# The attention part of y in DRAM, the pool part added by DMAs that add, and y's tiles lent to other rings

## The chip, the cores and the metric

The kernel runs on one core of a Trainium2 chip. The metric is the device time of one execution in microseconds (us); each kernel is judged by the median of its runs. Each core has five engines that take their instructions in order and meet at semaphores: TensorE (PE; its weight loads are listed as PEld), VectorE (DVE), ScalarE (ACT), GpSimd (POOL) and SyncE (SP), which here only issues DMAs. GpSimd issues some DMAs on a queue of its own.

## The reference

A DeepNorm decoder layer on 2048 rows of 1024 features, in float32. What matters here is its second half: an attention branch and a pooling branch, each projected to 1024 features, gated by sigmoids, added, projected again and normalised.

```python
  u = x * (1 + scale) + shift
  [q | k | v | a_gate | p_in | p_gate | m_a | m_p] = u @ W_in
  a = (attention(q, k, v) * silu(a_gate)) @ W_attn_proj
  p = (group_linear(causal_pool(p_in)) * pool_scale * silu(p_gate)) @ W_pool_proj
  y = sigmoid(m_a) * a + sigmoid(m_p) * p
  y = (y @ W_out) * (1 + gate)
  x = layer_norm(alpha * x + y)
```

## The kernel before

**How a product is made.** Every float32 operand is split into a high half that TensorE takes exactly and a low half, and a product is three: high by high, high by low, low by high (`mm3`). On top of that, two by two blocks of each large product are multiplied by a scheme with seven products in place of eight. A `Quad` is one such block: two weight tiles as the stationary side (loaded into `W` and `A22`, combined on GpSimd in `sum1`, `mid` and `late`, split by `pair_split` and `half_split` with the high half on ScalarE, L315, and the low half on VectorE, L131), and seven prepared "sets" B11, T1, T2, B21, T3, B22, T4 as the moving side. One product is 12 matmuls of 128x512, so a quad is 84 matmuls. `front` makes B11 and T1 of a quad, `back` the rest; the sums of products (u2, p5, c12) are made on VectorE and GpSimd (L366, L387). Four times in a quad a finished 128x512 result goes to the quad's `consume`, with (mi, t) saying which of the two weight tiles and which half of 1024 rows it belongs to.

**Stages.** Gates are computed first (stages g0 and g1, one for each half s of the rows) and written to DRAM, among them `ma_d` (sigmoid of m_a) and `mp_d`. Attention of a half follows each (a0 and a1); its result is stored as sets `ain_d` in DRAM. The last stage, called mix, starts with what was opened in a1 and has five phases: attention projection of s=0, pool projection of s=0, both again for s=1 (four quads each, in two groups of two), and the output projection with the normalisation of rows (eight quads).

**Tiles of the mix stage.** `Pools("mix", spare=2, p=4, c=5)` gives rings of 128x512 tiles (c with five places, p with four) and of 128x1024 tiles (spare with two). Eight tiles `wide0` to `wide7` of 128x1024 hold the attention part of y for the eight feature tiles, `ta[k]`; `wide4` to `wide7` are taken at the stage's start. In the output phase the same wide tags hold gain, bias and rows of x.

**Consumers.** `attn_quad` takes a place of ring c for the gate (ga), loads it on SP (L541), and VectorE multiplies the product by it into the half of `ta[k]` (L544). `pool_quad` loads its gate (gp, L551), VectorE multiplies in place (L552), GpSimd adds it to `ta` (L554), and GpSimd's queue stores the sum to `y_d` (L556), with 512-byte rows. Output quads load rows of `y_d` as their weights.

**Order of work.** Instructions written through `sp`, `act`, `dve`, `pool` and `pe` keep the order of the program on their engine; those through `nc.sync`, `nc.vector`, `nc.scalar` and `nc.gpsimd` are placed by a scheduler. A `tick` is called once per product; `defer(n, f)` runs f n ticks later, and `hooks` name work by group and tick. `set_steps` spreads the loading (SP, into a spare tile) and splitting (ACT and DVE) of the next phase's sets over fourteen half sets at the ticks of `SPLIT_AT`, with two loads ahead of the splits.

Of the kernel before, what the change touches and what calls it, by code (L numbers as in the profile page):

```python
# [2 lines left out]

# [1 line left out]

# [13 lines left out]
P = 128  # L19
# [39 lines left out]
def kernel(  # L59
# [84 lines left out]
    class Pools:  # L144


        def __init__(self, name, **bufs):
            self.name, self.bufs = name, bufs

        def __enter__(self):  # L150
            self.stack = ExitStack()
# [14 lines left out]
            return wp.tile([P, D], F32R, tag="wset", bufs=4, name="w_set")  # L166

        def spare(self, dt=F32):
            return self.t.tile([P, D], dt, tag="spare", bufs=self.bufs["spare"], name="spare")

        def c(self, name="c", dt=F32, tag="c"):
            return self.t.tile([P, CH], dt, tag=tag, bufs=self.bufs[tag], name=name)

        def p(self, name):
# [90 lines left out]
    class Quad:  # L265
# [1 line left out]

        def __init__(self, srcs, consume):  # L270
            self.srcs, self.consume = srcs, consume

        def load(self, ph, own, q=nc.sync, e=nc.gpsimd):
            self.w, self.a22 = ph.weights(), ph.last(own)
# [77 lines left out]
    def back(ph, grp, opened, nxt, own, tick, b22_first=False):  # L352
        st = []
        for q, (a, b, c, w) in zip(grp, opened):
            u2, p5 = ph.p("u2"), ph.p("p5")
            nc.scalar.copy(u2, a)
            nc.scalar.copy(p5, b)
            if w is None:
                w = pair_split(ph, q.second())
                q.late()  # L360
            if c is None:
                c = bank("lg")
                product(c, w[1], "T2", True)
            tick()
            nc.vector.tensor_tensor(u2, c, u2, ALU.add)  # L365
            nc.gpsimd.tensor_tensor(p5, p5, u2, ALU.add)  # L366
# [10 lines left out]

        def third(x):
            w[x] = pair_split(ph, st[x][0].third())
            if x < len(nxt):  # L380
                ask(nxt[x])

# [25 lines left out]
                with_b22(x)  # L408
        for q in nxt[len(st) :]:
            ask(q)  # L410
        for q, b, c, u2, p5 in st:
            w = half_split(ph, q.a22)
            product(c, w, "T4")
            tick()
            nc.vector.tensor_tensor(u2, c, u2, ALU.add)  # L415
            q.consume(ph, 1, 0, u2)
# [3 lines left out]
    def defer(ticks, f):  # L420
        due.append((now[0] + ticks, len(due), f))
# [48 lines left out]
    def set_steps(ph, store):  # L470


        if store["B11"].shape[0] == 4:
            return [(p, lambda n=n, h=h: fill_set(n, h, store[n])) for p, n, h in PLAN]
        raw, todo = {}, []

        def fetch(k):
            name, half = PLAN[k][1:]
            raw[k] = ph.spare()
            sp.dma_start(raw[k], store[name][half].rearrange("p a b -> p (a b)"))  # L480

        def split(k):
            name, half = PLAN[k][1:]
            split_set(name, 2 * half, by_two(raw[k]), 2, (act, dve))

        for k, at in enumerate(SPLIT_AT):
            if k < 2:
                todo.append((0, lambda k=k: fetch(k)))
            todo.append((at, lambda k=k: split(k)))
            if k + 2 < len(SPLIT_AT):  # L490
                todo.append((at, lambda k=k: fetch(k + 2)))
        return todo

    def planned(hooks, ph, store, last, pending={}):
# [39 lines left out]
    def wide(ph, i):  # L534
        return ph.t.tile([P, D], F32, tag=f"wide{i}", bufs=1, name=f"wide{i}")

    def attn_quad(s, m):
        def consume(ph, mi, t, src):
            k = m + mi
            g = ph.c("ga")  # L540
            nc.sync.dma_start(g, gates_d["ma"][s, k, t])  # L541
            if k not in ta:
                ta[k] = wide(ph, k)
            nc.vector.tensor_tensor(ta[k][:, t * CH : (t + 1) * CH], src, g, ALU.mult)  # L544

        return Quad((wap[m], wap[m + 1]), consume)

    def pool_quad(s, m):
        def consume(ph, mi, t, src):
            g = ph.c("gp")  # L550
            nc.sync.dma_start(g, gates_d["mp"][s, m + mi, t])  # L551
            nc.vector.tensor_tensor(g, src, g, ALU.mult)  # L552
            dst = ta[m + mi][:, t * CH : (t + 1) * CH]
            nc.gpsimd.tensor_tensor(dst, g, dst, ALU.add)  # L554
            k = 8 * s + 4 * t
            nc.gpsimd.dma_start(  # L556
                y_d[k : k + 4, :, m + mi, :].rearrange("s p q -> p s q"), dst.rearrange("p (s q) -> p s q", s=4)
            )

        return Quad((wpp[m], wpp[m + 1]), consume)  # L560

    zs = {}

# [756 lines left out]
        opened = attention(ph, 1, q0, (ain0_d, attn0[0]))  # L1320
    kv_stack.close()

    ta, vec = {}, {}
    with Pools("mix", spare=2, p=4, c=5) as ph:
        late_sets(ph.t, "T3", "T4")
        for k in range(4, KT):
            ta[k] = wide(ph, k)
        phases = []
        for s in range(2):
            phases.append((pairs(lambda m, s=s: attn_quad(s, m)) if s else attn0, ain_d[s]))  # L1330
# [3 lines left out]
        for i, (groups, store) in enumerate(phases):  # L1334
# [79 lines left out]
```

## Time and profile before

| | us |
|---|---|
| median of 3 runs | 1825.05 |
| lowest and highest | 1823.41 and 1826.09 |
| the profiled execution | 1824.69 |
| its span | 1822.9 |
| mean granted TensorE clock | 0.983 of full speed |

The span is what the profiler's rows cover. A row of the page names an engine, its busy time, its share of the span and its count of instructions. A row of the timeline gives a start, the time it took, the engine, the line, the operation with its tiles (output, arrow, inputs), a count, and in brackets the idle time before it and what ended that. A row of a group gives the sum and mean of its instructions and the idle time ahead of them. A row of DMA issues names the transfer, the queue that issues it, the count, the size of one and the median time from issue to landing. A row of waits names the instruction that waited, what it waited for, the total, the number of times and the longest.

### The profile page before, as it was taken

To read this page: it belongs to the slowest core of one execution; us is meant where nothing else is said; L and a number is where in the kernel's file an instruction comes from. 1 tells how busy PE (TensorE), PEld (TensorE's weight loads), DVE (VectorE), ACT (ScalarE), POOL (GpSimd) and SP (SyncE) were. 2 spreads that over 40 slices of the span, in tenths; PEclk is the share of its full clock that TensorE was granted. 3 is DMA by queue.
4 is the path that set the end of the run, shared out by engine and by line. 5 is a ranking of instruction groups with operands and counts; after the bars stand their busy time and mean duration, and the time that the engine had idled before them with its cause. 6 is when DMAs were issued, how large, how long until landed. Compare 5 with 4: busy or idle time off the path is not lost. (4 is left out here: it accounts for less than half of the span.)

```text
span 1822.9 us, 25301 instructions
## 1 busy us (share of the span) xinstructions
PE 1722.4 (94%) x8248; PEld 1432.9 (79%) x8248; DVE 1315.4 (72%) x2290; ACT 933.8 (51%) x1965; POOL 929.5 (51%) x758
## 2 busy tenths in 40 slices
PE   6789899999999999999999999999989999999996
PEld 6678787878888887777777888888877778777775
DVE  6967676644777787787666467777848897877887
ACT  4644344445777776444444377777724343423451
POOL 2245454551356567635445125357744875576552
PEclk9899999999999999999999999999999999999998
DMA  9265667656344468676676724453876575688442
GB/s 358 94 213 184 224 218 236 241 208 168 122 162 145 165 223 299 234 262 242 243 262 236 254 80 148 156 172 129 300 271 220 196 254 184 211 312 349 150 156 87
DMA packets 164003, 381.32 MB, mean 209 GB/s; under 512 B 19728, under 2 KB 23840, under 8 KB 163872
## 3 DMA queue, kind: packets, MB, share of 16 engines
q1 hardware_dynamic: 150528, 342.17, 53.7%
q0 software_dynamic: 10112, 33.06, 5.2%
q10 hardware_dynamic: 3232, 4.49, 0.9%
q8 instruction: 65, 1.06, 0.2%
q14 instruction: 66, 0.54, 0.1%
HBM read 244.35 MB, written 138.44 MB: 210 GB/s over the span
## 5 line engine op out<-in xcount | busy, mean ns | idle before, releaser
L55 PE MATMUL mm<-set_B,w_set 128*128 128x512 f32 x3240 | 802.1, 396 | 22.2 <-DVE w_set L131 22.0
L55 PEld LDWEIGHTS mm<-set_B,w_set 128*128 128x128 f32 x3240 | 602.9, 189 | 154.0 <-DVE w_set L131 30.3
L55 PE MATMUL lg<-set_T,w_set 128*128 128x512 f32 x2088 | 521.9, 400 | 44.3 <-DVE w_set L131 16.7
L55 PEld LDWEIGHTS lg<-set_T,w_set 128*128 128x128 f32 x2088 | 396.0, 192 | 146.2 <-DVE w_set L131 27.0
L131 DVE TENSOR_TENSOR w_set<-W,w_set 128x1024 fp32r<-128x1024 f32 x162 | 241.9, 1493 | 130.3 <-ACT w_set L315 125.6
L315 ACT CAST w_set<-W 128x1024 fp32r<-128x1024 f32 x162 | 169.2, 1049 | 242.5 <-PE mm L55 134.1
L55 PE MATMUL mm<-set_T,w_set 128*128 128x512 f32 x1080 | 266.4, 395 | 0.0
L55 PEld LDWEIGHTS mm<-set_T,w_set 128*128 128x128 f32 x1080 | 201.3, 189 | 41.6
L293 POOL TENSOR_TENSOR W<-W 128x512 f32<-128x512 f32 x56 | 80.0, 1429 | 151.0 <-DVE w_set L131 142.3
L287 POOL TENSOR_TENSOR W<-W 128x512 f32<-128x512 f32 x56 | 87.2, 1556 | 125.2 <-DVE w_set L131 99.9
L366 POOL TENSOR_TENSOR p<-p,u 128x512 f32<-128x512 f32 x58 | 100.6, 1736 | 87.3 <-DVE u L365 79.4
L55 DVE TENSOR_TENSOR o<-pv,o 64x128 f32<-64x128 f32 x256 | 72.4, 283 | 93.2 <-ACT o L55 90.5
L55 ACT ACTIVATE L<-L,nm 128x257 f32<-128x257 f32 (+1 forms) x256 | 127.1, 498 | 8.4 <-DVE nm L55 3.3
L283 POOL TENSOR_TENSOR W<-W,A 128x512 f32<-128x512 f32 x56 | 82.7, 1476 | 86.9 <-DMA W<-in_win_dram 20.2
L55 DVE TENSOR_TENSOR k_lo<-spare,k_hi 128x512 fp32r<-128x512 f32 x88 | 92.4, 1058 | 47.8 <-ACT k_hi L55 24.0
L55 DVE CUSTOM_DVE_ANT_0 L<-lg,bt,nsink 128x256 f32<-128x256 f32 (+1 forms) x256 | 111.6, 473 | 5.3 <-PE lg L55 1.3
L288 POOL TENSOR_TENSOR W<-W 128x512 f32<-128x512 f32 x56 | 90.4, 1614 | 15.1 <-DMA W<-in_win_dram 12.3
L55 POOL TENSOR_TENSOR w_set<-W,w_set 128x1024 fp32r<-128x1024 f32 x14 | 33.7, 2405 | 122.8 <-ACT w_set L55 89.7
L55 POOL TENSOR_TENSOR p<-nxt,pg 128x512 f32<-128x512 f32 x32 | 41.3, 1291 | 104.6 <-DVE sm L55 104.6
L55 ACT COPY o<-pv 64x256 f32<-64x256 f32 x128 | 47.3, 370 | 82.3 <-PE pv L55 80.2
L55 DVE TENSOR_TENSOR ptl<-pt,pth 128x512 fp32r<-128x512 f32 (+1 forms) x128 | 85.7, 669 | 1.7 <-ACT pth L55 1.6
L55 ACT CAST k_hi<-spare 128x512 fp32r<-128x512 f32 x88 | 53.4, 615 | 60.4 <-POOL spare L55 32.3
(207 smaller groups left out, 2507.2 us busy)
## 6 DMA issues: line engine op xcount, KB each, us to landing
W<-in_win_dram SPq DMA_DIRECT2D x68, 256.0 KB, 4.1
w_set<-wmix_d SPq DMA_DIRECT2D x32, 512.0 KB, 5.4
A<-in_win_dram SPq DMA_DIRECT2D x34, 256.0 KB, 5.1
W<-in_win_dram POOLq DMA_DIRECT2D x34, 256.0 KB, 3.6
ag_d<-sig SPq DMA_DIRECT2D x32, 256.0 KB, 3.5
pg_d<-sig SPq DMA_DIRECT2D x32, 256.0 KB, 3.6
ma_d<-sig SPq DMA_DIRECT2D x32, 256.0 KB, 4.1
mp_d<-sig SPq DMA_DIRECT2D x32, 256.0 KB, 3.7
```

The costliest lines, as they stand in the source:

```text
L55: return lambda *args, **kw: self.tc.keep_in_program_order(op(*args, **kw))
L131: engine.tensor_tensor(dst, src, as32(hi), ALU.subtract)
L283: e.tensor_tensor(self.w[:, 1, :], self.w[:, 2, :], self.a22, ALU.add)
L287: e.tensor_tensor(x[:, 1, :], x[:, 1, :], x[:, 0, :], ALU.subtract)
L288: e.tensor_tensor(x[:, 2, :], x[:, 0, :], x[:, 2, :], ALU.subtract)
L293: e.tensor_tensor(x[:, 0, :], x[:, 0, :], x[:, 1, :], ALU.subtract)
L315: a.copy(by_two(hi), raw)
L366: nc.gpsimd.tensor_tensor(p5, p5, u2, ALU.add)
```

## The change

The attention part of y no longer stays in SBUF. Both kinds of quad become one, `mixer_quad`. It loads the gate into a place of ring c (`gm`) with an ordered SP DMA at a time of its own, `ask`, which `Quad` now has beside `consume`: for result (0, 0) ahead of the T2 product, for the two results of t = 1 when the weights of T3 and B22 are split, and for (1, 0) ahead of the T4 products. `consume` multiplies the product by the gate in place. For attention it then stores the tile to `y_d` with a plain SP DMA two ticks later; for the pool part GpSimd's queue issues a DMA that adds the tile to what `y_d` holds (`accum_op=ALU.add`). The GpSimd add and `ta` are gone.

The eight wide tiles are lent: `wide0` to `wide3` to ring c, which so has nine places, taken in turn, and `wide4` to `wide7` to ring spare, which so has six. In the second pool phase, at tick 12 of its first group, the loan ends, and the tiles serve the output phase as before. The set loads run five ahead of the splits in place of two.

```diff
+        def lend(self, c, spare):
+            self.rooms = {"c": cycle(self.bufs["c"] * [None] + c), "spare": cycle(self.bufs["spare"] * [None] + spare)}
+
+        def room(self, ring):
+            return next(self.rooms[ring]) if self.rooms else None
...
         def spare(self, dt=F32):
+            tag = self.room("spare")
+            if tag:
+                return self.t.tile([P, D], dt, tag=tag, bufs=1, name="spare")
             return self.t.tile([P, D], dt, tag="spare", bufs=self.bufs["spare"], name="spare")
 
         def c(self, name="c", dt=F32, tag="c"):
+            room = self.room("c") if tag == "c" else None
+            if room:
+                return self.t.tile([P, D], dt, tag=room, bufs=1, name=name)[:, 0:CH]
             return self.t.tile([P, CH], dt, tag=tag, bufs=self.bufs[tag], name=name)
...
-        def __init__(self, srcs, consume):
-            self.srcs, self.consume = srcs, consume
+        def __init__(self, srcs, consume, ask=None):
+            self.srcs, self.consume, self.ask = srcs, consume, ask or (lambda *a: None)
...
                 w = pair_split(ph, q.second())
                 q.late()
+            q.ask(ph, 0, 0)
             if c is None:
                 c = bank("lg")
                 product(c, w[1], "T2", True)
...
         def third(x):
             w[x] = pair_split(ph, st[x][0].third())
+            for mi in ((0, 1) if b22_first else (1, 0)):
+                st[x][0].ask(ph, mi, 1)
             if x < len(nxt):
                 ask(nxt[x])
...
         for q in nxt[len(st) :]:
             ask(q)
+        for q, *_ in st:
+            q.ask(ph, 1, 0)
         for q, b, c, u2, p5 in st:
             w = half_split(ph, q.a22)
             product(c, w, "T4")
...
         for k, at in enumerate(SPLIT_AT):
-            if k < 2:
-                todo.append((0, lambda k=k: fetch(k)))
+            if k < 5:
+                todo.append((k // 2, lambda k=k: fetch(k)))
             todo.append((at, lambda k=k: split(k)))
-            if k + 2 < len(SPLIT_AT):
-                todo.append((at, lambda k=k: fetch(k + 2)))
+            if k + 5 < len(SPLIT_AT):
+                todo.append((at, lambda k=k: fetch(k + 5)))
...
+    def mixer_quad(s, m, weights, name):
+        gates = {}
+
+        def ask(ph, mi, t):
+            g = gates[mi, t] = ph.c("gm")
+            sp.dma_start(g, gates_d[name][s, m + mi, t])
+
+        def consume(ph, mi, t, src):
+            g = gates.pop((mi, t))
+            nc.vector.tensor_tensor(g, src, g, ALU.mult)
+            k = 8 * s + 4 * t
+            dst = y_d[k : k + 4, :, m + mi, :].rearrange("s p q -> p s q")
+            part = g.rearrange("p (s q) -> p s q", s=4)
+            if name == "ma":
+                defer(2, lambda: sp.dma_start(dst, part))
+            else:
+                nc.gpsimd.dma_start(dst, part, accum_op=ALU.add)
+
+        return Quad((weights[m], weights[m + 1]), consume, ask)
...
     def attn_quad(s, m):
-        def consume(ph, mi, t, src):
-            k = m + mi
-            g = ph.c("ga")
-            nc.sync.dma_start(g, gates_d["ma"][s, k, t])
-            if k not in ta:
-                ta[k] = wide(ph, k)
-            nc.vector.tensor_tensor(ta[k][:, t * CH : (t + 1) * CH], src, g, ALU.mult)
-
-        return Quad((wap[m], wap[m + 1]), consume)
+        return mixer_quad(s, m, wap, "ma")
 
     def pool_quad(s, m):
-        def consume(ph, mi, t, src):
-            g = ph.c("gp")
-            nc.sync.dma_start(g, gates_d["mp"][s, m + mi, t])
-            nc.vector.tensor_tensor(g, src, g, ALU.mult)
-            dst = ta[m + mi][:, t * CH : (t + 1) * CH]
-            nc.gpsimd.tensor_tensor(dst, g, dst, ALU.add)
-            k = 8 * s + 4 * t
-            nc.gpsimd.dma_start(
-                y_d[k : k + 4, :, m + mi, :].rearrange("s p q -> p s q"), dst.rearrange("p (s q) -> p s q", s=4)
-            )
-
-        return Quad((wpp[m], wpp[m + 1]), consume)
+        return mixer_quad(s, m, wpp, "mp")
...
-    ta, vec = {}, {}
+    vec = {}
     with Pools("mix", spare=2, p=4, c=5) as ph:
         late_sets(ph.t, "T3", "T4")
-        for k in range(4, KT):
-            ta[k] = wide(ph, k)
+        ph.lend(["wide0", "wide1", "wide2", "wide3"], ["wide4", "wide5", "wide6", "wide7"])
...
-            if i in (2, 4):
-                ta.clear()
             if i == 3:
...
+                hooks.setdefault((0, 12), []).append(lambda: ph.lend([], []))
                 hooks.setdefault((-1, 5), []).append(vectors)
                 hooks.setdefault((-1, 7), []).append(lambda: [load_z(ph, row) for row in range(2)])
```

More of the change, by code (lines that the diff above doesn't have):

```diff
@@ L2 @@
 from contextlib import ExitStack
+from itertools import cycle
 import numpy as np
@@ L148, in __init__ @@
             self.name, self.bufs = name, bufs
+            self.rooms = None
+        def lend(self, c, spare):
+            self.rooms = {"c": cycle(self.bufs["c"] * [None] + c), "spare": cycle(self.bufs["spare"] * [None] + spare)}
+        def room(self, ring):
+            return next(self.rooms[ring]) if self.rooms else None
         def __enter__(self):
```

## The prediction

> **What bounds the kernel now.** I read the page's busy shares first, then busy times by stage, then TensorE's timeline inside the stage that the change touches, then who holds up what TensorE waits for. The profiled execution took 1824.69 us (span 1822.9, so 1.8 around it), 0.36 below the median of the runs shown; the sum below is made against 1824.69 and nothing is added for that 0.36.
>
> ```profile
> PE 1722.4 (94%) x8248; PEld 1432.9 (79%) x8248; DVE 1315.4 (72%) x2290; ACT 933.8 (51%) x1965; POOL 929.5 (51%) x758
> ```
>
> TensorE is busy 94%, so a change that touches no matmul can only take from the remaining 6% and from clock lost. The diff lies in the last stage alone. Its attention phase s=0 ends at 1394.96, its pool phase at 1481.05, the attention and pool phases of s=1 at 1561.49 and 1642.81, and the output projection near 1801.60. In the windows the columns are stretch, length, busy time of PE, PEld, DVE, ACT, POOL, granted clock, DMA share, GB/s.
>
> ```profile
> 1325.51:1394.96 69.45, 64.02 (x268) 51.41 (x266) 43.12 (x48) 22.19 (x26) 31.08 (x22) 0.95 0.70 252
> 1394.96:1481.05 86.09, 79.01 (x336) 63.89 (x337) 77.60 (x63) 33.10 (x39) 63.69 (x50) 0.98 0.65 221
> 1481.05:1561.49 80.44, 78.08 (x336) 64.12 (x337) 65.08 (x63) 32.63 (x39) 43.69 (x30) 0.98 0.60 208
> 1561.49:1642.81 81.32, 77.44 (x334) 62.15 (x335) 65.78 (x54) 24.71 (x30) 56.91 (x47) 1.00 0.77 273
> 1642.81:1801.60 158.79, 150.70 (x651) 122.62 (x650) 124.12 (x159) 65.45 (x98) 85.11 (x66) 0.99 0.52 194
> ```
>
> Each middle phase is 336 matmuls. What would they take without a gap? TensorE's timeline has a run of twelve groups of 12 with no idle time between them:
>
> ```profile
> 1325.51 11.42 PE L55 MATMUL mm<-set_B,w_set 128*128 128x512 f32 x48
> 1336.76 5.60 PE L55 MATMUL lg<-set_T,w_set 128*128 128x512 f32 x24
> 1346.01 8.69 PE L55 MATMUL lg<-set_T,w_set 128*128 128x512 f32 x24 [3.65 <-ACT w_set L315]
> 1354.55 2.88 PE L55 MATMUL mm<-set_B,w_set 128*128 128x512 f32 x12
> ...
> 1387.18 5.60 PE L55 MATMUL lg<-set_T,w_set 128*128 128x512 f32 x24
> 1394.96 2.60 PE L55 MATMUL mm<-set_B,w_set 128*128 128x512 f32 x10 [1.72 <-DVE w_set L131]
> 1436.27 3.63 PE L55 MATMUL mm<-set_B,w_set 128*128 128x512 f32 x10 [2.35 <-DVE w_set L131]
> 1474.74 2.98 PE L55 MATMUL lg<-set_T,w_set 128*128 128x512 f32 x12 [1.62 <-DVE p L387]
> 1481.05 3.98 PE L55 MATMUL mm<-set_B,w_set 128*128 128x512 f32 x10 [2.88 <-DVE w_set L131]
> 1561.49 2.60 PE L55 MATMUL mm<-set_B,w_set 128*128 128x512 f32 x10 [2.37 <-DVE w_set L131]
> ```
>
> From 1354.55 to 1387.18 is 32.63 us for 144 matmuls, 226.6 ns each, so a phase has a floor of 336 x 0.2266 = 76.1 us. Over it the first pool phase loses 86.09 - 76.1 = 10.0, the attention phase of s=1 4.3, the second pool phase 5.2. Those 19.5, and the start of the stage (gap 3.65, then 24 matmuls in 8.69 where the same 24 take 5.60 at 1387.18: 6.7 together), are all that the change can win: 26 us. Nearly every gap is ended by VectorE, by the low half of a weight split (L131) or a product sum (L387): VectorE is late, though busy only some 80 to 90% of a phase.
>
> **Why VectorE is late** has two parts in the trace. The first is GpSimd's adds:
>
> ```profile
> 1619.14 1.23 DVE L131 TENSOR_TENSOR w_set<-W,w_set 128x1024 fp32r<-128x1024 f32 x1 [6.35 <-ACT w_set L315]
> 1626.67 5.75 DVE L131 TENSOR_TENSOR w_set<-W,w_set 128x1024 fp32r<-128x1024 f32 x1 [0.22 <-ACT w_set L315]
> 1626.30 1.30 POOL L366 TENSOR_TENSOR p<-p,u 128x512 f32<-128x512 f32 x1
> 1627.55 1.29 POOL L283 TENSOR_TENSOR W<-W,A 128x512 f32<-128x512 f32 x1
> 1628.80 1.29 POOL L554 TENSOR_TENSOR wide<-gp,wide 128x512 f32<-128x512 f32 x1
> 1630.05 1.28 POOL L288 TENSOR_TENSOR W<-W 128x512 f32<-128x512 f32 x1
> ```
>
> The same subtraction takes 1.23 alone and 5.75 while GpSimd runs four tensor operations end to end; it ends when they do. One of the four is the add L554, which the change removes; its price over all is in the group row, and what L131 takes in the phases with and without many of these adds is in the windows of that line (stretch, length, busy and count):
>
> ```profile
> L554 POOL TENSOR_TENSOR wide<-gp,wide 128x512 f32<-128x512 f32 x32 | 47.3, 1479 | 9.3 <-DVE gp L552 8.9
> 1394.96:1481.05 86.09, 29.35 (x16) 0.98 0.65 221
> 1481.05:1561.49 80.44, 22.08 (x16) 0.98 0.60 208
> 1561.49:1642.81 81.32, 33.21 (x16) 1.00 0.77 273
> ```
>
> L131 averages 1.83 us in the first pool phase and 2.08 in the second, against 1.38 in the attention phase between them. If both pool phases fall to 1.38, VectorE saves 16 x 0.45 = 7.3 and 16 x 0.70 = 11.1 us on this line alone. The second part is late gates and a blocked SP queue:
>
> ```profile
> DVE wide L544 <- DMA ga<-ma_d: 13.7, 7, 4.3
> SPq L55 <- DVE set_B L55: 61.6, 18, 13.4
> SPq L55 <- DVE set_T L55: 48.5, 18, 5.5
> ```
>
> VectorE stood 13.7 us waiting for attention gates (7 times), asked for only at the moment of use, behind 110 us in which SP waited for a spare tile of the next set to be split.
>
> **The change part by part.**
>
> *Removed: 32 adds on GpSimd (47.3 us), and the adds' wait.* GpSimd is not on the chain, so the gain is VectorE's. First pool phase: it loses 10.0; with 7.3 us less on L131 alone and the sums (L387) shortened too, I leave 2 us and take -8, between -3 (if L283, L288, L293 and L366 simply take the adds' place beside L131; 1626.67 shows that they also block) and -10 (the floor).
>
> *Gates asked earlier, rings of 9 and 6 tiles instead of 5 and 2, set loads five ahead.* The diff issues each gate load at least one product ahead of its use and in SP's fixed order. SP's 110 us of waits on two spare tiles fall away with six, so these loads are no longer behind them. In attention s=1: loses 4.3, of which 2.88 at its head is L131 held by the adds of the pool phase before. I take -3.3, ends -4.3 and +1 (SP now carries 32 added stores that wait for VectorE two ticks after the product, and a gate load behind one is late if VectorE is).
>
> *Added: 32 plain stores of 256 KB on SP, and 32 accumulating DMAs on GpSimd's queue in place of 32 plain stores.*
>
> ```profile
> y_d<-wide POOLq DMA_DIRECT2D x13, 256.0 KB, 4.5
> y_d<-wide POOLq DMA_DIRECT2D x16, 256.0 KB, 6.2
> W<-y_d SPq DMA_DIRECT2D x4, 256.0 KB, 6.3
> 1600.00:1625.00 25.00, 23.78 (x103) 18.73 (x102) 17.13 (x15) 5.19 (x7) 18.85 (x17) 1.00 0.84 296
> 1650.00:1675.00 25.00, 23.24 (x102) 18.88 (x102) 15.83 (x16) 7.35 (x10) 13.82 (x12) 1.00 1.03 409
> ```
>
> The plain stores fall in attention phases with a DMA share of 0.60 to 0.70: 16 x 256 KB = 4.2 MB a phase, some 10 us at the 409 GB/s of the fullest stretch, so an eighth of a phase: cover enough, 0. Without it a store merely holds one of nine gate tiles longer. No row shows an accumulating DMA. Its landing is bounded below by a plain store's 4.5 and above by twice the other stretch's 6.2, 12.4 (read and write of the destination one behind the other). In the first pool phase either end is hidden by nine places. In the last group of the second they are not: the wide tiles go back for gain, bias and rows of x, the gate ring is 5 again, and each place is held until its DMA lands. Queued behind: on SP, the loads of gain and bias wait for the accumulating DMAs that last held wide0 and wide1, behind them the last gates and the weight loads of the first output quads; on VectorE, the last c12 waits for a place, and behind it stands the low half of the first output quad's weights, which TensorE waits for. Near 4.5 to 6 us that costs nothing, at 12.4 some 6 us. I take 8, nearer to 6.2, since the destination rows move in the same packets: 2 us. Second pool phase: 5.2 lost, -4 by L131's smaller share, +2 for this: -2, ends -5 and +6. (The Trainium skill, "Collectives: The Full Stack", section "The bandwidth ceiling: the fold count and why AG ≠ RS ≠ AR", has an add in the DMA read two sources per chunk through one ring, and so half the rate; that speaks for the upper end and is weighed as the first rival.)
>
> *The start of the stage.* The wide tiles were the first that the stage took; now it takes them late, so the first tile is u2, and its place overlaps tiles of the attention stage that were still being stored. The first copy (L371, L356 before), which ran at 1322.27 with nothing to wait for, must wait for those stores:
>
> ```profile
> 1322.27 0.59 ACT L356 COPY u<-mm 128x512 f32<-128x512 f32 x1
> 1325.81 3.90 POOL L55 TENSOR_TENSOR a<-a,a 128x512 f32<-128x512 f32 x3
> 1327.13 2.93 SPq L55 DMA_DIRECT2D ain_T<-a  x3
> 1331.17 0.42 SPq L541 DMA_DIRECT2D ga<-ma_d  x1
> ain_T<-a SPq DMA_DIRECT2D x3, 256.0 KB, 2.0
> ```
>
> The store of T4's part is the middle one of three issued from 1327.13 to 1330.06, so issued about 1328.5, landed about 1330.5, copied by 1331.1. Behind this copy on ScalarE stand three more copies and the next weight splits; TensorE needs it for B21, which ran at 1325.51. So a new gap of 5.7 us, and if the clock falls as it did behind the 3.65 gap, 3.1 more: 8.8. Against it the old 6.7 go if the gates, whose first load was issued at 1331.17 behind those stores, come in time now. +2.1 with all of the clock, -1.0 with none. I take 0, ends -3 (copies granted sooner) and +4 (half of the old gap remains).
>
> *Everything else.* Into the output projection: set loads come earlier and the DMA share there is 1.03 already, so I put 0, ends -1.5 and +3. Because SP and VectorE are ordered anew over the whole stage, and a plan of 926 SP rows in place of 893 has new places to stand, I allow +3 for waits that I haven't seen (the largest single gap at present is about that).
>
> Sum: 0 - 8 - 3.3 - 2 + 0 + 3 = -10.3, so 1824.7 - 10.3 = 1814.4 us. The terms' ends, taken in root-sum, make the forecast's own range 1807 to 1821.
>
> **The rivals.**
>
> *Slower: accumulating DMAs land late in the last pool group.* Place: the ring of 5 at 1600 to 1645. For it: DMA share 0.84 there and 1.03 after it, where another 16 x 256 KB of reads at 409 GB/s are 10 us, half of them in the full stretch (+5). Price: at a landing of 12.4 the ring of 5 turns twice in a group, +6.2, and the first output weights, loaded from y_d behind the accumulations in a transfer of 6.3, start +6.2 later. With 0 - 8 - 3.3 + 5 + 12.4 = +6.1: 1831. It decides from about 10 us of landing; below that the five places turn within a product or two. Against: plain stores of the same shape land in 4.5 to 6.2 even in these stretches. By the skill's half rate, this is the case.
>
> *Less: the other GpSimd work fills the gap.* L131 is held by whatever GpSimd runs; in the phases with 3 adds it still averages 1.38, over its 1.23. If the sums of weights bunch up against the splits instead, the pool phases gain 4 rather than 10 and the start costs its +2.1: about 1822. Against: GpSimd's busy time falls from 63.69 by 20 in the first pool phase.
>
> *The change doesn't do what it says: gates still late.* The ordered loads stand on SP behind stores that wait for VectorE and behind the set loads; then the 13.7 us stay and the start has both gaps (+9 with the old one kept), against -8: about 1826. Against: nine places, and asks at least a product ahead.
>
> **How the numbers follow.** Forecast 0.52; less 0.14; late gates 0.08; slow accumulation, with any other cause of a slower time, 0.26. A difference of 0.2%, 3.65 us, is about what a measurement of this kernel can tell from no change. Faster: the forecast and two thirds of "less", with some of the rest, 0.62; same: the rest of "less" and most of "late gates", 0.11; slower: 0.27. Predicted 1814 us; range 1805 to 1830, low by the -10 and -4.3 ends together, high by the first rival. As cases of both signs hold much of the chance, the likeliest one's own range is 1807 to 1821.
>
> **What would show it.** Right: L131 near 1.4 us in the pool phases and gaps in the first pool phase under 3 us in sum; no wait on ma gates beyond the stage's start; a TensorE gap of about 5.7 us near 1325.5; accumulating DMAs landing in 6 to 9 us. Wrong: landings over 10, TensorE gaps ended by VectorE near 1625 to 1660 with VectorE waiting for a gate tile, SP standing on gain's load; or L131 still near 1.8 to 2.1 with the other GpSimd sums beside it; or gate waits on VectorE that have stayed.

## The result, and the profile after

The changed kernel takes 1835.18 us (median of 8 runs, 1831.33 to 1841.19); the kernel before, run beside it, 1825.90 (8 runs, 1821.35 to 1828.12). The ratio is 1.0056, interval 1.0040 to 1.0072: slower by some 10 us, where 1814 and a range of 1805 to 1830 were forecast. The profiled execution took 1836.81, span 1835.0.

```profile
PE 1725.9 (94%) x8248; PEld 1434.5 (78%) x8248; DVE 1292.6 (70%) x2290; ACT 931.4 (51%) x1965; POOL 895.9 (49%) x726
```

In the page's busy row GpSimd has lost 34 us and VectorE 23, as the change meant them to (GpSimd less than the 47.3 of the adds, for a reason that experiment 1 shows). The time is longer all the same, so TensorE must wait elsewhere.

**Where to measure from.** The code ahead of the mix stage is the same in both kernels, yet TensorE reaches the last ten matmuls of the second T2 product, just ahead of the stage, at 1323.11 before and at 1326.26 after. No engine's order differs ahead of that place, so I put these 3 us down to the execution and not to the change (in other executions below the same place is reached as late as 1335); one trace of the kernel before can't prove it. So I compare the stage from that place to the end of the last matmul, cut where each phase's first weights come in (in TensorE's timeline, the row of 10 matmuls that follows a row of 2 at a phase's head). In us, with the kernel of the first experiment in the last column:

| | before | after | plain stores |
|---|---|---|---|
| attention s=0 | 71.9 | 75.1 | 74.2 |
| pool s=0 | 86.1 | 86.4 | 80.3 |
| attention s=1 | 80.4 | 81.6 | 79.1 |
| pool s=1 and first output group | 125.2 | 125.4 | 117.8 |
| the other three output groups | 120.3 | 124.3 | 122.6 |
| the stage | 483.9 | 492.8 | 473.9 |

The windows of the changed kernel, with the columns of the prediction's: stretch, length, busy PE, PEld, DVE, ACT, POOL, clock, DMA share, GB/s. As in the prediction's windows, the second pool phase ends here where the first output group begins.

```profile
1401.40:1487.82 86.42, 81.14 (x336) 65.71 (x336) 63.40 (x63) 33.23 (x39) 53.33 (x38) 0.94 0.86 229
1487.82:1569.38 81.56, 77.04 (x336) 62.84 (x336) 65.81 (x63) 32.61 (x39) 38.05 (x26) 1.00 0.79 247
1569.38:1647.21 77.83, 76.73 (x337) 62.91 (x337) 55.34 (x52) 22.57 (x28) 45.80 (x35) 1.00 0.94 253
```

VectorE's 77.6 us of the first pool phase are 63.4, and that phase is no shorter. What rose is the DMA share, from 0.65 to 0.86, at nearly the same bytes a second (221 and 229). The same three stretches for the low halves of the splits alone (L132 now, L131 before):

```profile
1401.40:1487.82 86.42, 21.00 (x16) 0.94 0.86 229
1487.82:1569.38 81.56, 20.41 (x16) 1.00 0.79 247
1569.38:1647.21 77.83, 20.48 (x16) 1.00 0.94 253
```

1.31, 1.28 and 1.28 us each; the prediction had 1.38 for the pool phases. TensorE's timeline shows what took the place of that wait:

```profile
1334.35 13.62 PE L56 MATMUL mm<-set_B,w_set 128*128 128x512 f32 x48 [4.10 <-ACT u L371]
1401.40 3.97 PE L56 MATMUL mm<-set_B,w_set 128*128 128x512 f32 x10 [3.62 <-DVE w_set L132]
1456.44 5.89 PE L56 MATMUL lg<-set_T,w_set 128*128 128x512 f32 x12 [4.84 <-ACT w_set L330]
1499.94 0.74 PE L56 MATMUL lg<-set_T,w_set 128*128 128x512 f32 x2 [1.40 <-ACT w_set L330]
1665.40 1.66 PE L56 MATMUL mm<-set_B,w_set 128*128 128x512 f32 x6 [1.28 <-DMA set_B<-wo_B_split]
1668.25 2.56 PE L56 MATMUL lg<-set_T,w_set 128*128 128x512 f32 x10 [0.53 <-DVE w_set L132]
1679.15 1.66 PE L56 MATMUL mm<-set_B,w_set 128*128 128x512 f32 x6 [1.54 <-DMA set_B<-wo_B_split]
```

At 1456.44 there is a new gap of 4.84 us, and the 12 matmuls behind it take 5.89 instead of 2.88. At 1499.94 is a smaller one of the same kind. From 1665 on TensorE waits for the sets of the output phase, for which it had no such wait before. The chain of waits (start, length, what) leads from the gaps at 1456, 1499 and 1668 back to these DMAs:

```profile
1435.87 3.84 POOL y_d L574 x3
1441.34 13.91 DMA W<-in_wpp_dram
1455.35 1.05 ACT w_set L330
...
1489.83 8.92 DMA W<-in_wap_dram
...
1626.79 4.26 DMA W<-y_d
1631.05 12.22 DMA y_d<-gm
1644.24 6.62 DMA W<-y_d
```

A 256 KB weight load, issued on GpSimd's queue right behind adding DMAs, took 13.91 us, and one of the next phase 8.92; and the first output weights wait for an adding DMA that took 12.22. For the first pool phase, the row of GpSimd's DMA queue (packets, MB, share of the 16 engines) and rows of DMA issues (queue, count, size, median to landing):

```profile
q0 software_dynamic: 6754, 4.25, 34.9%
...
y_d<-gm POOLq DMA_DIRECT2D x14, 256.0 KB, 10.1
...
W<-in_wpp_dram POOLq DMA_DIRECT2D x4, 256.0 KB, 8.7
W<-in_wpp_dram SPq DMA_DIRECT2D x4, 256.0 KB, 4.0
```

Loads of the same weights land in 4.0 on SP's queue and in 8.7 on GpSimd's. In the kernel before, the same phase's row for GpSimd's queue was

```profile
W<-in_wpp_dram POOLq DMA_DIRECT2D x4, 256.0 KB, 3.6
```

The adding DMAs of the second pool phase, all 16, and then the last three, which the window from 1647 on has alone:

```profile
y_d<-gm POOLq DMA_DIRECT2D x16, 256.0 KB, 8.5
...
y_d<-gm POOLq DMA_DIRECT2D x3, 256.0 KB, 14.9
```

With plain stores (experiment 1) the last three land in 6.8.

### The profile page after: what moved, and what is told of

Same layout as the page of the kernel before. It is cut to its first block, busy times and chain, and to the rows that moved or that the text cites. A ratio compares the mean times of both kernels' runs of the same rounds, so it can differ in the third digit from the quotient of the medians.

```text
span 1835.0 us, 25284 instructions
## 1 busy us (share of the span) xinstructions
PE 1725.9 (94%) x8248; PEld 1434.5 (78%) x8248; DVE 1292.6 (70%) x2290; ACT 931.4 (51%) x1965; POOL 895.9 (49%) x726
## 3 DMA queue, kind: packets, MB, share of 16 engines
q0 software_dynamic: 24448, 33.06, 7.7%
## 4 chain that ended last, share of the span: by engine, by line
PE 30%; DMA 10%; DVE 8%; issue 5%; POOL 4%; ACT 2%; SPq 1%; POOLq 0%; DVEq 0%; ACTq 0%
PE mm L56 19%; PE lg L56 8%; DVE w_set L132 3%; PE pv L56 2%; DMA W<-in_wpp_dram 2%; PE pt L56 2%; DMA W<-y_d 1%; DMA W<-in_win_dram 1%; POOL W L302 1%; ACT w_set L330 1%; POOL spare L56 1%; DMA A<-y_d 1%; DVE k_lo L56 1%; DMA A<-in_win_dram 1%; DMA y_d<-gm 1%
## 5 line engine op out<-in xcount | busy, mean ns | idle before, releaser
L132 DVE TENSOR_TENSOR w_set<-W,w_set 128x1024 fp32r<-128x1024 f32 x162 | 219.8, 1357 | 161.4 <-ACT w_set L330 156.5
L308 POOL TENSOR_TENSOR W<-W 128x512 f32<-128x512 f32 x56 | 78.8, 1408 | 172.8 <-DVE w_set L132 164.4
L302 POOL TENSOR_TENSOR W<-W 128x512 f32<-128x512 f32 x56 | 88.7, 1583 | 124.1 <-DVE w_set L132 102.1
L298 POOL TENSOR_TENSOR W<-W,A 128x512 f32<-128x512 f32 x56 | 87.3, 1558 | 102.1 <-DMA W<-in_win_dram 22.9
L303 POOL TENSOR_TENSOR W<-W 128x512 f32<-128x512 f32 x56 | 85.8, 1532 | 17.5 <-DMA W<-in_win_dram 13.1
L56 POOL TENSOR_TENSOR w_set<-W,w_set 128x1024 fp32r<-128x1024 f32 x14 | 33.7, 2406 | 122.6 <-ACT w_set L56 89.7
L56 ACT COPY o<-pv 64x256 f32<-64x256 f32 x128 | 47.3, 370 | 80.8 <-PE pv L56 78.6
```

The costliest lines, as they stand in the source:

```text
L56: return lambda *args, **kw: self.tc.keep_in_program_order(op(*args, **kw))
L132: engine.tensor_tensor(dst, src, as32(hi), ALU.subtract)
L298: e.tensor_tensor(self.w[:, 1, :], self.w[:, 2, :], self.a22, ALU.add)
L302: e.tensor_tensor(x[:, 1, :], x[:, 1, :], x[:, 0, :], ALU.subtract)
L303: e.tensor_tensor(x[:, 2, :], x[:, 0, :], x[:, 2, :], ALU.subtract)
L308: e.tensor_tensor(x[:, 0, :], x[:, 0, :], x[:, 1, :], ALU.subtract)
```

## The experiments

Ratios are to the kernel before, run beside each, with a 95% interval; 0.1% is 1.8 us. A difference of two ratios is uncertain by some 0.2 to 0.3%, 4 to 6 us. The stage's length is measured as in the table above, in one execution of each kernel.

**1. Plain stores.**

```diff
-                nc.gpsimd.dma_start(dst, part, accum_op=ALU.add)
+                nc.gpsimd.dma_start(dst, part)
```

> Edit: the pool part is stored by a plain DMA on GpSimd's queue instead of one that adds, so y_d holds the pool part alone; the order of every engine is that of the changed kernel. Theory A (the adding DMAs are the loss: they land late, and hold up the mid loads behind them on GpSimd's queue and the wo sets and y_d weights beside them): landings of y_d stores fall from 8.5 to 10 us to 4.5 to 6.5, the 4.84 us gap at 1456 goes with its slow clock (-7), the first output group gives back its 4.4: about 1824 us. Rival B (it is the 32 added transfers, SP's new order and the five-deep set loads): within 3 us of the changed kernel's 1835.

The plain store overwrites the attention part, so y_d holds the pool part alone. Measured: 0.9949 (0.9931 to 0.9967), the stage 473.9, 19.0 shorter than the changed kernel's. No engine's order differs from the changed kernel's, so the difference of the two ratios, 0.0107 or 19.5 us (give or take 4), is the price of adding in the DMA. The gap at 1456 is gone (the first pool phase 80.3), and so are the waits for output sets. The queue's row over the whole run, of this kernel and then of the changed one:

```profile
q0 software_dynamic: 10112, 33.06, 5.3%
```
```profile
q0 software_dynamic: 24448, 33.06, 7.7%
```

The same 33.06 MB. 5.3% of 1821.2 us is 96.5 us of all 16 engines, 7.7% of 1835.0 is 141.3. The difference over 32 DMAs is 1.40 us each; a plain 256 KB at the queue's own rate (96.5 us for 33.06 MB) is 0.77. So by an estimate from these shares the packets of an adding DMA took some 2.17 us of all 16 engines, 2.8 times a plain one's. (This is packet time, not time in which nothing else moves: the DMA share, made of such times, reaches 1.03 in a window that the prediction shows.) There were 512 data packets where the plain one had 64: 14336 more on the queue, 448 each, and the page counts 16384 more packets of under 2 KB, 512 each.

GpSimd's time for the issuing itself also rose. Its group rows (count, sum and mean), of the changed kernel and of this one:

```profile
L574 POOL DMA_DIRECT2D y_d<-gm x32 | 41.5, 1349 | 14.0 <-DVE gm L567 13.4 <-issue 0.4
```
```profile
L574 POOL DMA_DIRECT2D y_d<-gm x32 | 24.3, 761 | 14.6 <-DVE gm L567 9.1 <-DVE w_set L132 1.9 <-DMA W<-y_d 1.6
```

1.35 us each in place of 0.76, 17 us in sum; three of these (3.84 us) stand ahead of the late load on the chain above. The 19.5 us are the price of all this together: engines, queue and issuing.

**2. The loads behind them moved to SP.**

```diff
-        def mid(self, q=nc.gpsimd, e=nc.gpsimd):
-            x = self.w
+        def mid(self, q=None, e=nc.gpsimd):
+            x, q = self.w, q or self.mid_q
...
+        if name == "mp" or s == 1:
+            q.mid_q = nc.sync
```

> Edit: the late weight loads (mid) of the pool quads and of the attention quads of s = 1 are issued on SP instead of GpSimd's queue, where the adding DMAs are. If the 4.84 us gap of the first pool phase is a load queued behind adding DMAs: it goes, -5 to -8, 1827 to 1830, and these loads land in some 4 us instead of 8.7. If the DMA engines themselves are full: the loads land as late as before, and the time stays within 2 us of 1835. A third way: SP is held by other waits when the load should be issued, and the gap moves there.

Measured: 1.0038 (1.0025 to 1.0051), the stage 488.2: 3 us better by the ratios, whose intervals overlap, and 4.6 by the stage. On SP the loads land in 3.8 us in the first pool phase, and that phase takes 82.3 in place of 86.4. But TensorE's timeline has

```profile
1487.90 4.64 PE L56 MATMUL mm<-set_B,w_set 128*128 128x512 f32 x10 [3.89 <-DVE w_set L132]
1667.27 1.66 PE L56 MATMUL mm<-set_B,w_set 128*128 128x512 f32 x6 [1.14 <-DMA set_B<-wo_B_split]
```

a gap of 3.89 at the next phase's head, where the changed kernel had 0.40, and the waits for the output's sets as before. So queueing behind the adding DMAs is a part, the first theory's, and the gap moved, as in the third way; what the rest is, this run doesn't show.

**3. The start of the stage put back.**

```diff
+        for k in range(4, KT):
+            wide(ph, k)
         ph.lend(["wide0", "wide1", "wide2", "wide3"], ["wide4", "wide5", "wide6", "wide7"])
```

> Edit: wide4 to wide7 are taken first when the stage opens, as before the change, so that u2 no longer lies where attention tiles are still being stored. Theory: the 4.10 us TensorE gap at 1334 and its slow clock go, and nothing takes their place since the gates were asked for early: -5 to -8 us, 1827 to 1830. Rival: the gates and the T3 and T4 sets are not there in time either, and a gap of 3 to 4 us opens some 12 us later as it did before the change: -1 to -3.

Measured: 1.0061 (1.0041 to 1.0080), no different from the changed kernel, where the theory gave 5 to 8 us and the rival 1 to 3. The copy of u2 runs at 1334.38 now, with no wait ahead of it, and yet the first attention phase only falls from 75.1 to 73.5. VectorE's timeline, then TensorE's:

```profile
1345.35 0.69 DVE L567 TENSOR_TENSOR gm<-mm,gm 128x512 f32<-128x512 f32 x1 [6.62 <-DMA gm<-ma_d]
1345.96 2.35 DVE L132 TENSOR_TENSOR w_set<-W,w_set 128x1024 fp32r<-128x1024 f32 x2
```
```profile
1347.22 6.91 PE L56 MATMUL mm<-set_B,w_set 128*128 128x512 f32 x22 [3.40 <-DVE w_set L132]
1362.29 4.42 PE L56 MATMUL lg<-set_T,w_set 128*128 128x512 f32 x18 [1.35 <-DMA set_T<-ain_T_split]
```

The first gate arrives 6.62 us after VectorE wants it, and the split behind that multiplication holds TensorE 3.40 us: the rival's mechanism. In the changed kernel the start's own gap hid this lateness.

**4. Set loads two ahead.** In `set_steps` every 5 becomes 2 and `k // 2` becomes 0, as before the change.

> Edit: set loads two ahead of the splits, as before the change, in place of five. Theory A (adding DMAs): within 3 us of 1835, either way. Rival B (the five-deep loads fill the DMA engines just when weights are wanted): 3 to 6 us faster, and the DMA share of the first attention and pool phases falls from 0.92 and 0.86 towards 0.8.

Measured: 1.0093 (1.0068 to 1.0119), slower by 7 us than the changed kernel, which neither theory gave. TensorE's timeline has the gap behind the adding DMAs longer, and another in the next phase:

```profile
1461.05 5.49 PE L56 MATMUL lg<-set_T,w_set 128*128 128x512 f32 x12 [7.02 <-ACT w_set L330]
1509.09 0.73 PE L56 MATMUL lg<-set_T,w_set 128*128 128x512 f32 x2 [3.79 <-ACT w_set L330]
```

So the five-deep loads aren't the loss; without them the kernel is slower, though the two intervals just touch.

**5. Rows of 2 KB.** `y_d` gets the part itself as its unit; the output quads gather rows of 512 bytes when they load.

```diff
-    y_d = dp.tile([S // P, P, KT, P], F32, name="y_d")
+    y_d = dp.tile([4, KT, P, NB, P], F32, name="y_d")
...
-            dst = y_d[k : k + 4, :, m + mi, :].rearrange("s p q -> p s q")
-            part = g.rearrange("p (s q) -> p s q", s=4)
+            dst, part = y_d[2 * s + t, m + mi].rearrange("p s q -> p (s q)"), g
...
+                v = y_d[src // 4, 4 * half : 4 * half + 4, :, src % 4, :].rearrange("k p q -> p k q")
+                q.dma_start(dst.rearrange("p (k q) -> p k q", k=4), v)
```

> Edit: y_d is laid out so that a stored part has rows of 2 KB in place of 512 bytes; the output quads' weight loads then read rows of 512 bytes. Everything is still computed. Theory (the price of an adding DMA is its packets: 512 of 512 bytes each, where the plain DMA on the same queue had 64 of 4 KB): 128 packets each now, landings of 8.5 to 10 us fall to 4 to 6, the loads behind them too, 8 to 15 us faster than the changed kernel: 1820 to 1827. Rival (the price is the reading and adding of 256 KB, whatever the packets): landings stay over 8, and the time within 4 us of 1835, or above it by the output loads in small rows.

Measured: 1.0013 (0.9998 to 1.0028), 7.9 us better than the changed kernel, the stage 481.1. The queue's row on the page, and the rows of DMA issues for the adding DMAs of the first and the second pool phase:

```profile
q0 software_dynamic: 12160, 33.06, 6.8%
```
```profile
y_d<-gm POOLq DMA_DIRECT2D x15, 256.0 KB, 7.5
...
y_d<-gm POOLq DMA_DIRECT2D x16, 256.0 KB, 7.6
```

128 packets each (64 plain + (12160 - 10112) / 32), and 6.8% of 1826.0 us is 124.2: 27.7 over the plain stores, 0.86 each, so 1.63 us of all engines, still 2.1 times plain. GpSimd's issuing takes 0.92 us each:

```profile
L580 POOL DMA_DIRECT2D y_d<-gm x32 | 27.9, 916 | 16.3 <-DVE gm L575 13.1 <-DVE c L421 2.3 <-issue 0.8
```

Both theories hold in part: some 8 of the 19.5 us (give or take 4) came with the 512 small packets. The other 11.7 stay, with 1.63 us of engine time against 0.77, landings of 7.5 against 6.6 with plain stores, and only 3.6 us more of GpSimd than they have. (The Trainium skill, "Collectives: The Full Stack", section "The bandwidth ceiling: the fold count and why AG ≠ RS ≠ AR", says of a ReduceScatter that its add reads two sources and so runs at half the rate of a copy; the 2.1 here, of one core's DMAs, is close to that.)

**6. Rows of 2 KB, and the loads on SP.** As 5 and 2 together, and also `q.mid_q = nc.sync` for the first two output quads.

> Edit: the rows of 2 KB, and the late weight loads of the pool quads, of the attention quads of s = 1 and of the first output group on SP. If packets were the price, nothing is left for the queue behind them: within 3 us of the kernel with 2 KB rows alone. If bytes were: 3 to 5 us faster than that kernel, as the move alone was against the changed kernel.

Measured: 1.0040 (1.0026 to 1.0054), 5 us slower than the rows alone, which neither way had expected. TensorE's timeline, then SP's, then the chain of waits:

```profile
1666.12 5.67 PE L56 MATMUL lg<-set_T,w_set 128*128 128x512 f32 x12 [7.65 <-ACT w_set L339]
```
```profile
1646.29 2.58 SPq L212 DMA_DIRECT2D set_B<-wo_B_split  x2
```
```profile
1649.28 15.66 DMA W<-y_d
```

One gap of 7.65: ScalarE waits for a load from `y_d` that took 15.66 us. On SP's queue it stood right behind two set loads of 1 MB, issued from 1646.29. Here moving a load from one queue to another only traded what was ahead of it.

**7. Plain stores, and GpSimd's adds again.**

```diff
+                nc.gpsimd.tensor_tensor(g, g, g, ALU.add)
                 nc.gpsimd.dma_start(dst, part)
```

> Edit: on the kernel with plain stores in place of adding ones, GpSimd again adds a 128x512 tile ahead of each pool store (the tile to itself, so y_d holds twice the pool part and no attention part). Theory (the adds' time beside VectorE's splits and sums was worth some 8 us in the first pool phase and less in the others): 6 to 12 us slower than the plain stores' 0.995 of before, so 0.998 to 1.001, with L131's successor (L132) back near 1.8 us in the pool phases. Rival (the earlier gates and the longer rings were the gain): within 3 us of the plain stores' time.

Each add is of the tile to itself, so y_d holds twice the pool part and no attention part. Measured: 1.0030 (1.0018 to 1.0043), 0.0081 or 14.8 us over the plain stores (give or take 4), above the upper end expected. VectorE, ScalarE and SP keep the plain stores' order, and GpSimd has the 32 adds more, so this is the adds' price. Windows of this kernel, then of the plain stores, first and second pool phase:

```profile
1408.32:1496.97 88.65, 80.59 (x337) 64.61 (x337) 74.32 (x63) 33.17 (x40) 64.25 (x52) 0.96 0.65 226
1578.76:1658.70 79.94, 77.12 (x335) 62.65 (x336) 63.73 (x54) 22.54 (x28) 57.06 (x49) 1.00 0.72 253
```
```profile
1405.64:1485.90 80.26, 79.05 (x336) 64.91 (x336) 62.02 (x63) 33.34 (x39) 45.61 (x38) 0.97 0.71 251
1564.97:1641.00 76.03, 76.03 (x329) 62.85 (x330) 53.41 (x54) 22.66 (x28) 41.44 (x36) 0.98 0.75 270
```

GpSimd's extra 18.6 and 15.6 us come back as 12.3 and 10.3 on VectorE, which has as many instructions as with plain stores: VectorE's are stretched beside GpSimd's. L132 itself rose only to 1.42 and 1.64 us, less than the 1.8 expected, so the rest of it lies on VectorE's other operations.

**8. Each part stored twice, plainly.** Of experiment 1, with another store of the same tile ahead of it:

```diff
+                nc.gpsimd.dma_start(y2_d[k : k + 4, :, m + mi, :].rearrange("s p q -> p s q"), part)
                 nc.gpsimd.dma_start(dst, part)
```

> Edit: on the kernel with plain pool stores, each pool part is stored twice by GpSimd's queue, first to a tensor that nothing reads, then to y_d (no adding, so y_d holds the pool part alone). Engine time worked out from the queue's shares: a plain store 0.77 us of all 16 engines, an adding one with 512-byte rows 2.17, with 2 KB rows 1.63; two plain stores make 1.54. Theory (what an adding DMA costs is the time it fills the engines and the queue): the time comes out near that of the kernel with 2 KB rows, 0.998 to 1.003 of before. Rival (the adding itself holds things up in a way that traffic doesn't, such as the wait for the landing): within 3 us of the plain stores, 0.994 to 0.997.

Measured: 1.0019 (1.0003 to 1.0036). The queue's row gives 6.5% of 1827.9 us = 118.8, so 22.3 over the single stores or 0.70 for each second one. With no adding at all, the same kind of gaps come back:

```profile
1453.02 0.73 PE L56 MATMUL lg<-set_T,w_set 128*128 128x512 f32 x2 [1.96 <-ACT w_set L331]
1651.12 0.73 PE L56 MATMUL mm<-set_B,w_set 128*128 128x512 f32 x2 [1.42 <-ACT w_set L331]
1673.45 1.65 PE L56 MATMUL mm<-set_B,w_set 128*128 128x512 f32 x6 [0.73 <-DMA set_B<-wo_B_split]
```

So most of a loss of this size comes without any adding: 0.0070 or 12.8 us over the single stores. A second store also takes GpSimd some 24 us in sum to issue (0.76 us each), and this run can't part that from the time in the engines. Experiment 5 can: 3.6 us more of GpSimd than the plain stores, 27.7 more of the engines, and 11.7 us slower.

**9. Plain stores, without the attention's.** `defer(2, lambda: sp.dma_start(dst, part))` becomes `pass`.

> Edit: on the kernel with plain pool stores, the 32 stores of the attention part on SP are left out. Theory (they lie in phases with room for them and cost nothing): within 3 us of the plain stores' 0.995 of before. Rival (they hold SP in its order and its loads behind VectorE): 4 us or more faster, 0.993 or less.

Measured: 0.9913 (0.9888 to 0.9938), 6.6 us below the plain stores, though the intervals overlap; the stage 470.6 against 473.9. The 32 added stores likely cost 3 to 7 us, which the prediction had at nothing. In the plain-store kernel SP stood 55.1 us, in 20 waits, in the first three phases for the products that these stores wait for, and in this one 0.5 us:

```profile
SPq L56 <- DVE gm L567: 55.1, 20, 18.6
```

**10. Three edits together, all computed.** Rows of 2 KB, the start of experiment 3, and the late loads on SP for the pool quads alone.

> Edit: rows of 2 KB, the wide tiles taken first at the stage's start, and the late weight loads of the pool quads alone on SP. Everything is computed. Against the kernel with 2 KB rows alone (1.0013 of before): the start was worth 1.7 us by the trace, the pool quads' loads some 2 where packets are fewer, so 0.998 to 1.000 of before. If the loads on SP move the gap to the next place, as a 7.65 us gap came when the output quads' loads moved too: 1.002 or more.

Measured: 0.9999 (0.9985 to 1.0013), as expected. It is the fastest of those that compute everything, and no faster than the kernel before.

**11. Half and half, all computed.** Of experiment 5 with the start of 3; the first tile of each pair stays in SBUF and is added on GpSimd, the second goes by the adding DMA. Ring c has five places.

```diff
+            if mi == 0 and name == "ma" and (s, m) not in ta:
+                ta[s, m] = wide(ph, m // 2)
+            own = ta[s, m][:, t * CH : (t + 1) * CH] if mi == 0 else None
...
+            if mi == 0:
+                if name == "mp":
+                    nc.gpsimd.tensor_tensor(own, g, own, ALU.add)
+                    nc.gpsimd.dma_start(dst, own)
```

> Edit: rows of 2 KB; of each two feature tiles the first keeps its attention part in SBUF (wide0 to wide3) and is added on GpSimd as before the change, the second goes by the adding DMA; ring c has five places, ring spare six, and the wide tiles for it are taken first. Everything is computed. Theory (VectorE is slowed only where its work on SBUF and GpSimd's together overfill a phase, and DMA traffic only where it overfills the engines, so half of each costs less than half): 1815 to 1823 by the scale of the first runs, 0.994 to 0.998 of before. Rival (both prices are in proportion): 0.999 to 1.002. A ring of five with gates asked early may also hold up SP: above 1.002.

Measured: 1.0063 (1.0043 to 1.0082), the last of the three cases. VectorE's waits in the stage:

```profile
DVE wide L578 <- DMA gm<-ma_d: 13.4, 4, 6.8
DVE c L421 <- DMA y_d<-gm: 7.4, 3, 4.2
```

The gates are late as before the change, and c12 waits for a place whose adding DMA hasn't landed: what the nine places were for. With the ring of five in it, this run can't decide between the theory and the rival.

## Why the prediction was wrong, point by point

In us against the kernel before, by the stage's phases, with the second pool phase cut from the output as in the windows:

| | forecast | measured | with plain stores |
|---|---|---|---|
| start and attention s=0 | 0 | +3.3 | +2.3 |
| pool s=0 | -8 | +0.3 | -5.8 |
| attention s=1 | -3.3 | +1.1 | -1.4 |
| pool s=1 | -2 | -3.5 | -5.3 |
| output | 0 | +7.7 | +0.2 |
| waits not seen | +3 | | |
| together | -10.3 | +8.9 | -10.0 |

**The price of an adding DMA** is the step that failed. It was put at a landing of 8 us, 2 us on the path, with all of it in the last pool group; the runs put it at 19.5 us. The ground given, that "the destination rows move in the same packets", was false: 512 packets in place of 64. The landing was nearly 8 in the second pool phase (8.5), but 10.1 in the first, 12.22 on the chain, and 14.9 for the last three, above the bound of 12.4. And the landing of the store itself was too narrow a measure: the packets of each took 2.17 us of all engines in place of 0.77, its issuing 1.35 us of GpSimd in place of 0.76, and what stood behind or beside it came late.

**"In the first pool phase either end is hidden by nine places"** was false. The nine places hid the landing from VectorE, but not from the late weight loads on the same queue: 8.7 us where SP's took 4.0, one of them 13.91, a gap of 4.84 with slow matmuls behind it. The diff leaves those loads where they were, and the prediction didn't look at what an edit puts ahead of others in a queue. This ate the phase's forecast -8, which plain stores show to be -5.8 otherwise.

**Attention s=1** was put at -3.3 and came out at +1.1. Part was a misreading: the gap of 2.88 taken to be at its head ends at 1481.05, so it lies in the first pool phase's window and was counted there too. What the phase itself lost was the slow clock behind that gap (10 matmuls in 3.98 us, 2.56 now) and the gap of 2.37 at its end, which stayed (2.60). Plain stores show -1.4. Most of the rest went into the gap at 1499.94, behind a load on GpSimd's queue that took 8.92 us.

**Into the output projection** was put at 0, ends -1.5 and +3. The second pool phase did better than its term, -3.5 against -2, but the first output group is 3.7 us longer than before and the other three 4.0. Together the second pool phase and the first output group are 7.6 us above the plain stores. The rival "accumulating DMAs land late" named the late landings and the late first output weights, and its 1831 is near the measured 1835, but in part by luck: it kept the -8 of the first pool phase, which was lost, and put +17.4 on the ring of five and the output weights, where the traces show some 7.6 over plain stores. Of the ring of five, VectorE waited for a place once, for 0.5 us, and SP stood 13.8 us for adding DMAs, 5.7 more than for plain stores. Its weight, 0.26, was too small: that plain stores land in 6.2 was no evidence on a DMA that adds.

**GpSimd's adds** were a right step, rightly sized. L132 fell to 1.3 us as forecast, VectorE by 14 and 10 us in the pool phases, and experiment 7 prices the adds at 14.8 us, where the prediction's terms make 8 and 4 for the pool phases and a part of the 3.3 for attention s=1. Had the adding been as cheap as a plain store, the kernel would have stood 9.3 us below the one before (0.9949), next to the forecast -10.3. That nearness is partly luck: by phase the plain stores miss the terms by 2 to 3 us both ways, and the +3 for waits not seen closes the sum.

**The start of the stage** was right: the copy waited 8.32 us for the store's landing, by ScalarE's timeline

```profile
1333.71 0.59 ACT L371 COPY u<-mm 128x512 f32<-128x512 f32 x1 [8.32 <-DMA ain_T<-a]
```

and B21 came 5.7 us later after the 3.15 of the execution are taken off (1334.35 - 1325.51 - 3.15). TensorE's gap is only 4.10, since the ten matmuls ahead of it, whose code the change leaves alone, took 3.99 us in place of 2.56; with plain stores they took 2.60 and the gap is 5.50. The phase lost 3.3, inside its ends of -3 and +4 but at the upper one. The late gates that the prediction hoped to be rid of were only covered by it, as experiment 3 shows.

**Nothing for the added stores** was likely wrong by 3 to 7 us (experiment 9), and the three later output groups are 4.0 us longer than before (2.3 with plain stores). Some 2.6 of it is the slow clock behind gaps of much the same length (rows of ten matmuls in 3.59 and 4.14 us where the kernel before has 2.56 twice; last section); the rest wasn't followed.

Together: -14.8 for the adds, +19.5 for adding by DMA, and some +5.5 for the rest (experiment 7 has the adds and the plain stores, and stands at 1.0030), in which stores, start, earlier gates and deeper loads stand against one another; experiments 3, 4 and 9 bear on them, within the noise of a ratio.

## What to carry to other kernels

Price a DMA that adds by the time its packets take of the engines and by the time its issuing takes, not by the landing of a plain one: here 2.8 times the engine time with rows of 512 bytes and 2.1 times with rows of 2 KB, and 1.35 or 0.92 us of GpSimd in place of 0.76. Then list what else is queued behind it and what shares the engines in the fullest stretch. Work taken off one resource that overfills a phase (here GpSimd's adds, worth 14.8 us) is only won if the resource it goes to has room in that very phase.

## What the runs showed of the hardware that was not expected

Plain stores with the same 512-byte rows made 64 packets of 4 KB on GpSimd's queue; adding made 512 of 512 bytes, and the layout alone, 128 packets, was worth 7.9 us. Small packets were dear only together with the adding: the attention's plain stores on SP's queue, with the same rows, made 512 of 512 bytes too (16384 such packets in the changed kernel's trace), and took 455 us of packet time, 0.89 us of all 16 engines each. The adding ones' 16384 packets took 1121 us there, 2.19 each, and with rows of 2 KB 801 us, 1.56 each.

The last ten matmuls ahead of the stage start at 1323.11 in the profiled execution of before and at 1335.37 in that of experiment 3, 12 us apart with no edit there. A single span can't tell 10 us here; the stage's own length and the paired ratios could.

The slow clock behind a short gap comes and goes. Two rows of TensorE's timeline, of the changed kernel and of experiment 3, at the same place of the output phase:

```profile
1779.60 4.14 PE L56 MATMUL mm<-set_B,w_set 128*128 128x512 f32 x10 [1.89 <-DVE w_set L132]
```
```profile
1786.32 2.57 PE L56 MATMUL mm<-set_B,w_set 128*128 128x512 f32 x10 [1.88 <-DVE w_set L132]
```

Gaps of 1.89 and 1.88 us; ten matmuls took 4.14 us behind the one, at a granted clock of 0.57, and 2.57 behind the other, at 1.00.
